# Output projection and first inner block of a two-layer diffusion step: other norm order, ScalarE copies, a third view, mask and sink

## The chip, the cores and the metric

The kernel runs on one core of one Trainium2 chip. TensorE (PE) multiplies, VectorE (DVE), ScalarE (ACT) and GpSimd (POOL) work elementwise, SyncE (SP) issues transfers. The metric is the device time of one execution in microseconds, median of several runs; the profile is of one execution more.

## The reference

One step of a two-layer backbone on 1024 latent tokens and 128 prompt tokens, width 1024, in float32. Layer 0 mixes tokens by differential attention (8 heads), layer 1 by sliding-window attention with a sink (16 heads in 4 groups); after each comes the output projection, a gated residual, and a SwiGLU feed-forward of 2816 inner columns. Cut to what the change touches:

```python
def post_norm_residual(x, y, g, gate):
    return x + gate * rmsnorm(y, g)

def pre_norm_modulate(x, g, shift, scale):
    return rmsnorm(x, g) * (1 + scale) + shift

def sink_softmax(s, sink):
    m = jnp.maximum(jnp.max(s, axis=-1, keepdims=True), sk)
    e = jnp.exp(s - m)
    return e / (jnp.sum(e, axis=-1, keepdims=True) + jnp.exp(sk - m))

ys = swa_latent_attention(...) @ w_o_swa[j]
xs = post_norm_residual(xs, ys, norm_g[i, 1], ms[2])
hs = pre_norm_modulate(xs, norm_g[i, 2], ms[3], ms[4])
y  = (jax.nn.silu(h @ w_gate) * (h @ w_up)) @ w_down
```

## The kernel before

Tokens stand in nine blocks of 128: eight latent ones and the prompt. Every float32 product is made of three matmuls on rounded parts: high x high, high x low, low x high. An operand is "split" by a cast (high) and a subtraction (low).

The order of instructions on each engine is the order of the code, which is written out by hand: a step function walks a tuple of actions, hooks put other work in between, and lists (`late`, `ahead`) say what follows which product. Each engine takes its own instructions in that order.

*Sliding-window attention* (`swa_attention`, from L981). At its start the mask is loaded (L986) and cast (L987), the identity cast (L989). A unit is one group of four heads and one token block. Per head: PE makes scores (L1014, L1017) and adds the mask by a matmul (L1020); VectorE takes the row maximum (L1025) and the minimum with the negated sink (L1026, 128x1); ScalarE takes the exponent (L1029); PE turns it (L1049); the turned tiles are split by ScalarE and VectorE, or, some of them, by POOL (rounding at L110, subtraction at L1072); PE multiplies by V (L1081, L1082).

*Output projection* (`OProj`, from L1237). `step(i)` handles five blocks at once at different ages: load x of block i, turn the heads of block i+1 (`turn`: PE transposes into PSUM, ScalarE copies them out, POOL rounds, VectorE subtracts, L1310 to L1316), statistics of the heads in layer 0 (L1263), the two halves of the projection of block i (`proj`, 24 matmuls each, L1324 to L1326, four PSUM tiles in turn), and for block i-1 the norms: `norms` 0 squares the projection, 1 makes the post-norm and the new x, stores x and squares it, 2 makes the pre-norm. The lines inside are those of helpers: L127 square with sum, L130 add, L135 root, L137 reciprocal, L153 and L154 post-norm, L145 and L146 pre-norm.

*Inner feed-forward blocks* (`Halves`, `Ffn`, `up`). The two halves of the input and the four of each weight are combined so that seven products per block of 128 inner columns do for gate and up: input combinations B11, B21, B22, T1 to T4 (`Halves`), weight combinations s0, s1 and so on (`prep`). The inputs of two token blocks form a pair: (0,4) and (1,5) make view 0 of 256 columns, (2,6), (3,7) and half of the prompt each side make view 1 of 320. `first` copies the turned first block out (ScalarE casts at L1393, VectorE copies at L1394), `second` makes the seven combinations of the second and splits them (L1404, L1407 are the helpers for high and low). `up` runs the inner blocks d = 0 to 21; d = 0 is written apart: seven products on view 0, with the pairs of view 1 prepared behind them, then seven on view 1. Each product is 12 matmuls (L1516 to L1518) into `guX`, `guY` or `guZ`, after which `sums` copies, adds and takes Silu (L1532 to L1553). `prep` for d = 0 is called by hooks at the last steps of the projection; there POOL makes s0 (L1468, L1469) and s1 (L1474, L1475) and the splits are at L1486 and L1488.

The lines that set the order in the projection and in the first block:

```python
for k, what, *arg in (
        (0, "load_x"), (1, "turn"), (3 - self.l, "load"), (-1, "norms", 0), (2, "stat", 0), (2, "stat", 1),
        (0, "proj", 0), *(((None, 0), (2, "scale")), ((None, 0), (2, "scale")))[self.l],
        (-1, "norms", 1), (-1, "norms", 2), (0, "proj", 1), (None, 1)):
...
late = [[], [lambda: step(pairs[0])], [lambda: step(pairs[0], 2), lambda: f.fetch(1)],
        [lambda: step(pairs[1])], [lambda: step(pairs[1], 2)], [], [lambda: step(pairs[2], 2)]]
```

Of the kernel before, what the change touches and what calls it, by code (L numbers as in the profile page):

```python
# [18 lines left out]
P = 128  # L19
# [25 lines left out]
def hybrid_step(ctx: ExitStack, tc: tile.TileContext, x_prompt, x_sample, cache_diff_k, cache_diff_v,  # L45
# [40 lines left out]
    negsink = const.tile([P, SH], F32, name="negsink")  # L86

# [354 lines left out]
    def small_params(sb):  # L442

        dma(out=subg, in_=diff_subln_g.rearrange("o p -> p o"))
# [536 lines left out]
    def swa_attention(op, wo_pool, pre, kv0, q0):  # L981
        with sbuf("sa") as sb, psum("sap") as ps:

            mask = sb.tile([P, 2, P], BF16, name="mask")
            mraw = sb.tile([P, 2, P], F32, name="mraw")
            dma(out=mraw, in_=swa_mask)  # L986
            act.copy(out=mask, in_=mraw)  # L987
            ident_b = sb.tile([P, P], BF16, name="ident_b")
            act.copy(out=ident_b, in_=ident)  # L989

            class Unit:
# [245 lines left out]
    class OProj:  # L1237
# [63 lines left out]
        def turn(self, tb):  # L1301
            i = OORDER.index(tb) % 2 * 2
            oh, ol = self.ohl[tb] = [self.room(f"w{i + f}", [P, KB, P], F32R, "oh") for f in range(2)]
            o32 = self.room("r1", [P, KB, P], F32, "o32")
# [23 lines left out]
        def norms(self, tb, part):  # L1328
# [4 lines left out]
            elif part == 1:  # L1333
# [3 lines left out]
                self.ss[tb] = sumsq([x], junk)  # L1337
# [24 lines left out]

    A_COLS = {(0, 0): ((0, 256, 0),), (0, 1): ((0, 256, 256),), (1, 0): ((0, 320, 512),),
              (1, 1): ((0, 256, 896), (256, 320, 832))}

    class Halves:
# [23 lines left out]
        def first(self, part, c, a, raw):  # L1390

            for i, name in enumerate(("B11", "B21")):
                act.copy(out=self.hi[name, part][:, :, c:c + a[i].shape[-1]], in_=a[i])  # L1393
                dve.tensor_copy(out=raw[:, i], in_=a[i])  # L1394

        def second(self, part, c, b, raws):
# [19 lines left out]
            high("B22", B22)  # L1416
            high("T2", T2)
            low("T3", T)
            dve.tensor_tensor(out=T, in0=B21, in1=T2, op=ALU.subtract)
            high("T4", T)  # L1420
            for name, x in (("B11", B11), ("B21", B21), ("T1", T1), ("T2", T2), ("B22", B22), ("T4", T)):
                low(name, x)
# [18 lines left out]
    class Ffn:  # L1441
# [18 lines left out]
        def prep(self, d, what):  # L1460
# [9 lines left out]
            elif what == "s1":  # L1470
# [3 lines left out]
                pool.tensor_tensor(out=s[:, 0:512], in0=A11, in1=A21, op=ALU.subtract)  # L1474
                pool.tensor_tensor(out=s[:, 512:D], in0=A12, in1=w[d, "r", "s0"][:, 512:D], op=ALU.subtract)  # L1475
            elif what == "u":
                u = w[d, "u"] = rooms.take((P, D), F32R, "fhl")
                act.copy(out=u[:, 0:512], in_=A22)
# [520 lines left out]
```

## Time and profile before

| | |
|---|---|
| median of 3 runs | 3180.54 us (3177.97 to 3180.6) |
| the profiled execution | 3179.54 us |
| its span | 3177.7 us |
| mean granted clock of PE | 0.982 |
| PE, DVE, ACT, POOL busy | 94%, 65%, 45%, 38% |

The profiled execution is 1.8 us longer than its span (start and end), and 1.0 us under the median. Stages follow each other: QKV product of layer 0 to 385 us, differential attention to 822, output projection to 968, up projection to 1500, down to 1795, then layer 1: QKV to 1960, sliding-window attention to 2234, output projection to 2366, up to 2891, down to the end. In a timeline row the columns are start, duration, engine, line, operation, output and inputs, shapes, and in brackets the idle time ahead of it with what ended it. The granted clock is a share of full speed: 1.00 is 2.4 GHz, the lower level 1.2 GHz.

### The profile page before, as it was taken

The page shows a single profiled execution, that of the slowest core. Times are in us where ns is not written, and L with a number is a line of the kernel's source. Part 1 is how long each engine was busy: PE and PEld are TensorE (multiplying, and loading weights), DVE is VectorE, ACT ScalarE, POOL GpSimd, SP SyncE. Part 2 cuts the span into 40 slices and gives each one's busy share as a digit, 9 for nine tenths or more (in the row PEclk, how much of TensorE's full clock was granted, in tenths as well). Part 3 has the DMA queues.
Part 4 walks back from the last instruction along what each step waited for, and adds up shares of the span by engine and source line. Part 5 has one row for each costly group of instructions (what it writes and reads, how often), then busy time and mean ns, then how long its engine had stood idle before and what let it go on. Part 6 is the DMA issues. An engine that isn't in the chain of part 4 may idle for free.

```text
span 3177.7 us, 47863 instructions
## 1 busy us (share of the span) xinstructions
PE 3000.0 (94%) x17998; PEld 2637.4 (83%) x17998; DVE 2070.7 (65%) x2849; ACT 1423.8 (45%) x2764; POOL 1215.6 (38%) x1120
## 2 busy tenths in 40 slices
PE   8999989988887999999999998999988999999999
PEld 5888777777776999999888787777768999998887
DVE  6786388888587777753786643999586633334544
ACT  6332267777554333333344323777443333333442
POOL 0453389999312444433000143666213434330000
PEclk9999999999898999999999999999999999999999
DMA  6675543332423343424865454433432322226664
GB/s 214 190 222 190 182 135 115 121 115 85 126 100 98 112 125 110 129 83 150 290 215 193 149 174 126 117 114 102 143 116 75 109 67 79 77 70 214 196 197 142
DMA packets 373807, 442.22 MB, mean 139 GB/s; under 512 B 26804, under 2 KB 295644, under 8 KB 373576
## 3 DMA queue, kind: packets, MB, share of 16 engines
q1 hardware_dynamic: 373576, 439.16, 43.9%
q8 instruction: 142, 2.33, 0.3%
q14 instruction: 89, 0.73, 0.1%
HBM read 335.71 MB, written 103.37 MB: 138 GB/s over the span
## 4 chain that ended last, share of the span: by engine, by line
PE 68%; POOL 13%; DVE 9%; ACT 4%; issue 3%; DMA 1%; SPq 1%; ACTq 0%; DVEq 0%; POOLq 0%
POOL aT L784 7%; PE guX L1516 6%; PE guX L1517 6%; PE guX L1518 6%; PE dacc L1633 6%; PE dacc L1635 6%; PE dacc L1634 6%; POOL aT L110 5%; PE qacc L556 4%; PE qacc L558 4%; PE qacc L557 4%; PE guY L1518 3%; PE guY L1516 3%; PE guY L1517 3%; PE guZ L1516 1%
## 5 line engine op out<-in xcount | busy, mean ns | idle before, releaser
L1633 PE MATMUL dacc<-fh,ahl 128*128 128x512 f32 x792 | 311.4, 393 | 2.4 <-DVE U L1552 2.4
L1635 PE MATMUL dacc<-fh,ahl 128*128 128x512 f32 x792 | 310.3, 392 | 0.0
L1634 PE MATMUL dacc<-fl,ahl 128*128 128x512 f32 x792 | 310.3, 392 | 0.0
L1549 POOL TENSOR_TENSOR sg<-sg,U 128x256 f32<-128x256 f32 x88 | 74.9, 851 | 576.2 <-ACT sg L1548 565.0
L556 PE MATMUL qacc<-whi,hh 128*128 128x512 f32 x648 | 259.3, 400 | 0.0
L558 PE MATMUL qacc<-whi,hl 128*128 128x512 f32 x648 | 254.3, 392 | 0.0
L557 PE MATMUL qacc<-wlo,hh 128*128 128x512 f32 x648 | 253.7, 391 | 0.6 <-DVE wlo L106 0.6
L617 POOL TENSOR_TENSOR qout<-t,t 128x512 f32<-128x512 f32 (+1 forms) x56 | 67.8, 1212 | 485.7 <-DVE vst L587 283.5
L784 POOL TENSOR_TENSOR aT<-a,aT 128x512 fp32r<-128x512 f32 x186 | 237.5, 1277 | 15.5
L1618 DVE TENSOR_TENSOR fl<-fraw,fh 128x1024 fp32r<-128x1024 f32 x132 | 161.7, 1225 | 118.6 <-ACT fh L1617 115.0
L744 DVE TENSOR_REDUCE nm<-S 128x1 f32<-128x1280 f32 x128 | 190.2, 1486 | 50.9 <-PE S L737 50.9
L1617 ACT CAST fh<-fraw 128x1024 fp32r<-128x1024 f32 x132 | 138.4, 1049 | 164.0 <-DMA fraw<-in_w_down_dram 157.4
L737 PE MATMUL S<-K,q 128*128 128x512 f32 (+1 forms) x768 | 184.5, 377 | 13.3 <-ACT e L749 9.2
L266 DVE SCALAR_TENSOR_TENSOR macc<-wmod,sc,macc 128x512 f32<-128x512 f32 x196 | 186.3, 994 | 0.0
L1633 PEld LDWEIGHTS dacc<-fh,ahl 128*128 128x128 f32 x792 | 148.7, 188 | 36.4 <-DVE U L1552 3.3
L1635 PEld LDWEIGHTS dacc<-fh,ahl 128*128 128x128 f32 x792 | 148.7, 188 | 33.5
L578 ACT CAST xT<-tpx 128x512 fp32r<-128x512 f32 x127 | 68.8, 591 | 240.2 <-issue 125.4
L1634 PEld LDWEIGHTS dacc<-fl,ahl 128*128 128x128 f32 x792 | 148.7, 188 | 32.8
L749 ACT ACTIVATE e<-S,nm 128x1280 f32<-128x1280 f32 x128 | 171.6, 1340 | 7.2 <-DVE nm L744 7.1
L737 PEld LDWEIGHTS S<-K,q 128*128 128x128 f32 x768 | 137.5, 193 | 44.3 <-ACT e L749 19.5
L110 POOL TENSOR_SCALAR aT<-a 128x512 fp32r<-128x512 f32 x192 | 154.2, 803 | 24.0 <-ACT a L773 24.0
L1488 DVE TENSOR_TENSOR fl<-fsum,fh 128x1024 fp32r<-128x1024 f32 x84 | 102.4, 1219 | 81.0 <-ACT fh L1486 81.0
(363 smaller groups left out, 9592.2 us busy)
## 6 DMA issues: line engine op xcount, KB each, us to landing
fraw<-in_w_down_dram SPq DMA_DIRECT2D x132, 512.0 KB
wmod<-in_w_mod_dram SPq DMA_DIRECT2D x112, 256.0 KB
araw<-a_d SPq DMA_DIRECT2D x132, 192.0 KB
fraw<-in_w_gate_dram SPq DMA_DIRECT2D x44, 512.0 KB
fraw<-in_w_up_dram SPq DMA_DIRECT2D x42, 512.0 KB
qT_d<-xT SPq DMA_DIRECT2D x36, 512.0 KB
q<-qT_d SPq DMA_DIRECT2D x64, 256.0 KB
wraw<-in_w_qkv_diff_dram SPq DMA_DIRECT2D x24, 512.0 KB
```

The costliest lines, as they stand in the source:

```text
L110: pool.tensor_scalar(out=out, in0=in_, scalar1=1.0, scalar2=0.0, op0=ALU.mult, op1=ALU.add)
L556: pe.matmul(acc, lhsT=xh, rhs=hi[:, a, :], start=(kb == 0), stop=False)
L557: pe.matmul(acc, lhsT=xh, rhs=lo[:, a, :], start=False, stop=False)
L558: pe.matmul(acc, lhsT=xl, rhs=hi[:, a, :], start=False, stop=(kb == KB - 1))
L737: pe.matmul(S[:, j:j + n], lhsT=self.q[:, f, m, i * P:(i + 1) * P], rhs=kv[self.h][0][:, m, j:j + n], start=(f == 0), stop=(f == 1))
L784: (dve if self.last else pool).tensor_tensor(out=lo, in0=x, in1=hi.bitcast(F32), op=ALU.subtract)
L1516: pe.matmul(o, lhsT=hi[:, kb, :], rhs=xh[:, kb, :], start=(first and kb == 0), stop=False, **more)
L1517: pe.matmul(o, lhsT=hi[:, kb, :], rhs=xl[:, kb, :], start=False, stop=False, **more)
L1518: pe.matmul(o, lhsT=lo[:, kb, :], rhs=xh[:, kb, :], start=False, stop=(kb == 3), **more)
L1633: pe.matmul(acc, lhsT=ah, rhs=hi[:, cs], start=(d == 0), stop=False)
L1634: pe.matmul(acc, lhsT=ah, rhs=lo[:, cs], start=False, stop=False)
L1635: pe.matmul(acc, lhsT=al, rhs=hi[:, cs], start=False, stop=(d == NDF - 1))
```

## The change

- *Norms.* `norms` has four parts. 0 and 1 stay one step behind the projection; the square of x (2) and the pre-norm (3) come at the start of the step after, two behind. Two more steps run at the end instead of code written out for the prompt.
- *Turn.* ScalarE writes the rounded high part straight from PSUM, VectorE subtracts it from PSUM; the copy o32 and POOL's rounding are gone.
- *Halves.* `first` only copies out, both copies on ScalarE; the casts of B11 and B21 stand in `second`, whose order changes.
- *Views.* In d = 0, view 1 of 320 columns is done as views of 256 and 64 columns; from d = 1 on nothing changes.
- *Prep.* For d = 0 VectorE makes s1 instead of POOL; hooks move; the fetch of d = 1 follows view 0.
- *Mask and sink.* Mask and bfloat16 identity are made with the small parameters in the QKV stage. The minimum with the sink takes the sink as a scalar operand.

```diff
     def small_params(sb):
+        mraw = junk[:, 0:2 * P].rearrange("p (a k) -> p a k", k=P)
+        dma(out=mraw, in_=swa_mask)
+        act.copy(out=mask, in_=mraw)
+        act.copy(out=ident_b, in_=ident)
...
-                    dve.tensor_tensor(out=nm, in0=nm, in1=negsink[:, hs:hs + 1], op=ALU.min)
+                    dve.tensor_scalar(out=nm, in0=nm, scalar1=negsink[:, hs:hs + 1], scalar2=None, op0=ALU.min)
...
         def turn(self, tb):
+                hi, lo = oh[:, ks, :], ol[:, ks, :]
                 if self.l == 0:
-                    act.activation(out=o32[:, ks, :], in_=tp, func=AF.Copy, scale=subg)
+                    act.activation(out=hi, in_=tp, func=AF.Copy, scale=subg)
+                    dve.scalar_tensor_tensor(out=lo, in0=tp, scalar=subg, in1=hi.bitcast(F32), op0=ALU.mult,
+                                             op1=ALU.subtract)
                 else:
-                    act.copy(out=o32[:, ks, :], in_=tp)
-                pool_round(oh[:, ks, :], o32[:, ks, :])
-                dve.tensor_tensor(out=ol[:, ks, :], in0=o32[:, ks, :], in1=oh[:, ks, :].bitcast(F32), op=ALU.subtract)
+                    act.copy(out=hi, in_=tp)
+                    dve.tensor_tensor(out=lo, in0=tp, in1=hi.bitcast(F32), op=ALU.subtract)
...
                 dma(out=x_d[tb * P:(tb + 1) * P, :], in_=x)
-                self.ss[tb] = sumsq([x], junk)
+            elif part == 2:
+                self.ss[tb] = sumsq([self.xt[tb]], junk)
...
-                    (0, "load_x"), (1, "turn"), (3 - self.l, "load"), (-1, "norms", 0), (2, "stat", 0), (2, "stat", 1),
-                    (0, "proj", 0), *(((None, 0), (2, "scale")), ((None, 0), (2, "scale")))[self.l],
-                    (-1, "norms", 1), (-1, "norms", 2), (0, "proj", 1), (None, 1)):
+                    (-2, "norms", 2), (-2, "norms", 3), (0, "load_x"), (1, "turn"), (3 - self.l, "load"),
+                    (-1, "norms", 0), (2, "stat", 0), (2, "stat", 1), (0, "proj", 0), (None, 0), (2, "scale"),
+                    (-1, "norms", 1), (0, "proj", 1), (None, 1)):
...
+    VIEWS = ((0, 0, 256), (1, 0, 320), (1, 0, 256), (1, 256, 320))
...
-            for i, name in enumerate(("B11", "B21")):
-                act.copy(out=self.hi[name, part][:, :, c:c + a[i].shape[-1]], in_=a[i])
-                dve.tensor_copy(out=raw[:, i], in_=a[i])
+            for i in range(2):
+                act.copy(out=raw[:, i], in_=a[i])
...
+            act.copy(out=B22, in_=b[1])
             dve.tensor_tensor(out=T1, in0=b[0], in1=B11, op=ALU.subtract)
-            act.copy(out=B22, in_=b[1])
             dve.tensor_tensor(out=T, in0=B22, in1=b[0], op=ALU.subtract)
+            high("B11", B11)
+            high("B21", B21)
             high("T1", T1)
...
-                pool.tensor_tensor(out=s[:, 0:512], in0=A11, in1=A21, op=ALU.subtract)
-                pool.tensor_tensor(out=s[:, 512:D], in0=A12, in1=w[d, "r", "s0"][:, 512:D], op=ALU.subtract)
+                eng = pool if d else dve
+                eng.tensor_tensor(out=s[:, 0:512], in0=A11, in1=A21, op=ALU.subtract)
+                eng.tensor_tensor(out=s[:, 512:D], in0=A12, in1=w[d, "r", "s0"][:, 512:D], op=ALU.subtract)
...
-                    for i, k in enumerate((0, 1, 2, 4, 3, 5, 6)):
-                        self.product(0, k, 0)
-                        for f in late[i] if i < len(late) else ():
-                            f()
-                    for k in range(7):
-                        self.product(0, k, 1)
-                        self.free(0, k)
-                        self.ahead(1, k)
+                    for view in (0, 2, 3):
+                        for i, k in enumerate((0, 1, 2, 4, 3, 5, 6)):
+                            self.product(0, k, view)
+                            if view == 3:
+                                self.free(0, k)
+                            for f in late.get((view, i), ()):
+                                f()
...
-                hooks[8, 0] = [lambda: prep("s0", "hg")]
-                hooks[8, 1] = [lambda: prep("s1", "lg")]
-                for i in range(-2, NTB):
+                hooks[8, 0] = [lambda: prep("s0", "hg", "lg")]
+                hooks[9, 0] = [lambda: prep("ha", "s1", "la")]
+                hooks[9, 1] = [lambda: prep("hb", "lb")]
+                for i in range(-2, NTB + 2):
...
+                late = {(0, 1): [pair(0)], (0, 4): [pair(0, 2)], (0, 5): [pair(1)],
+                        (0, 6): [pair(1, 2), lambda: f.fetch(1)], (2, 1): [pair(2, 2)],
+                        (2, 3): prep("s0"), (2, 4): prep("s1"), (2, 6): prep("hg"),
+                        (3, 1): prep("lg", "ha"), (3, 3): prep("la", "hb"), (3, 5): prep("lb"),
+                        (3, 6): prep("u") + [lambda: f.fetch(2)]}
```

The order on VectorE at the end of the projection of layer 0, where the last pair of view 0 ends and the post-norm of the block before the last follows. Before (K is the room of x, `oh` the low part of the turned heads, `xn` the normed block):

```order
L1407 TENSOR_TENSOR T2l<-raw,T2h 128x4x128
L1407 TENSOR_TENSOR B22l<-raw,B22h 128x4x128
L1407 TENSOR_TENSOR T4l<-raw,T4h 128x4x128
L1316 TENSOR_TENSOR oh<-o_9452,oh 128x512 x2
L130 TENSOR_TENSOR ss<-ss 128x1
L137 RECIPROCAL rs<-ss 128x1
L153 SCALAR_TENSOR_TENSOR xn<-oacc,rs,q 128x512 x2
L154 TENSOR_TENSOR K<-xn,K 128x1024
L137 RECIPROCAL rs<-ss 128x1
L145 SCALAR_TENSOR_TENSOR xn<-K,rs,bc 128x1024
L146 TENSOR_TENSOR xn<-xn,bc 128x1024
```

And now (the lines are shifted: L148 and L149 are the pre-norm, L156 and L157 the post-norm, L1312 the subtraction in `turn`):

```order
L1410 TENSOR_TENSOR T1l<-raw,T1h 128x4x128
L1410 TENSOR_TENSOR B22l<-raw,B22h 128x4x128
L1410 TENSOR_TENSOR T4l<-raw,T4h 128x4x128
L140 RECIPROCAL rs<-ss 128x1
L148 SCALAR_TENSOR_TENSOR xn<-K,rs,bc 128x1024
L149 TENSOR_TENSOR xn<-xn,bc 128x1024
L1312 SCALAR_TENSOR_TENSOR oh<-tp_o,subg,oh 128x512 x2
L133 TENSOR_TENSOR ss<-ss 128x1
L140 RECIPROCAL rs<-ss 128x1
L156 SCALAR_TENSOR_TENSOR xn<-oacc,rs,q 128x512 x2
L157 TENSOR_TENSOR K<-xn,K 128x1024
```

The pre-norm that followed a block's own post-norm now stands ahead of the next block's post-norm, and the subtraction of the heads reads PSUM.

The order on ScalarE in view 0 of layer 0, before (`s` and `U` are copies of sums out of PSUM, `fh` and `fhl` weight casts):

```order
L1486 CAST fh<-V 128x1024
L135 ACTIVATE ss<-ss,eps_t 128x1
L1532 COPY s_9709<-guX 128x256
L127 ACTIVATE junk,ss<-K 128x1024
L135 ACTIVATE ss<-ss,eps_t 128x1
L1478 CAST fhl<-V 128x512
L1393 CAST B11h<-tp_n 128x4x128
L1393 CAST B21h<-tp_n 128x4x128
L1537 COPY U_9752<-guX 128x256
L1538 ACT_TABLE_LOAD
L1538 ACTIVATE s_9709<-s_9709 128x256
```

And now:

```order
L1543 COPY s_9687<-guX 128x256
L138 ACTIVATE ss<-ss,eps_t 128x1
L1496 CAST fh<-K 128x1024
L1397 COPY raw<-tp_n 128x512 x2
L1548 COPY U_9728<-guX 128x256
L1549 ACT_TABLE_LOAD
L1549 ACTIVATE s_9687<-s_9687 128x256
L130 ACTIVATE junk,ss<-K 128x1024
L138 ACT_TABLE_LOAD
L138 ACTIVATE ss<-ss,eps_t 128x1
L1552 COPY U_9743<-guX 128x256
L1488 CAST fhl<-V 128x512
```

The casts straight from the turned tile became raw copies, and between Silu and the U copy stands a square and a root with a table load each way.

## Rows read from the trace of the kernel before

**Rows 1.** The page, part 1: busy time, share and instructions of each engine.

```profile
PE 3000.0 (94%) x17998; PEld 2637.4 (83%) x17998; DVE 2070.7 (65%) x2849; ACT 1423.8 (45%) x2764; POOL 1215.6 (38%) x1120
```

**Rows 2.** Table by stage: stretch, length, PE PEld DVE ACT POOL busy, clock, DMA, GB/s.

```profile
840.00:970.00 130.00, 115.92 (x546) 94.82 (x546) 99.59 (x164) 72.09 (x213) 19.45 (x17) 0.93 0.35 115
...
970.00:1030.00 60.00, 40.09 (x245) 38.19 (x245) 42.25 (x63) 26.12 (x49) 12.56 (x12) 0.83 0.25 77
...
1030.00:1500.00 470.00, 469.54 (x3503) 464.64 (x3503) 310.19 (x355) 157.53 (x297) 199.52 (x161) 1.00 0.38 115
...
1970.00:2234.00 264.00, 245.28 (x1663) 203.16 (x1664) 236.09 (x465) 198.16 (x468) 169.74 (x191) 0.99 0.37 109
...
2368.00:2430.00 62.00, 40.67 (x264) 39.09 (x265) 43.88 (x66) 25.81 (x49) 16.60 (x14) 0.83 0.25 76
```

**Rows 3.** Timeline of PE, output projection, both layers (idle before, releaser).

```profile
934.12 1.97 PE L1386 MATMUL tp_n<-ident,xn 128*128 128x128 f32 x8 [3.11 <-DVE raw L1394]
...
954.84 0.77 PE L1324 MATMUL oacc<-woh,oh 128*128 128x512 f32 x1 [4.49 <-DVE xn L153]
...
2353.26 0.76 PE L1324 MATMUL oacc<-woh,oh 128*128 128x512 f32 x1 [5.16 <-DVE xn L153]
```

**Rows 4.** Timeline of PE, first inner block of both layers.

```profile
977.37 0.89 PE L1386 MATMUL tp_n<-ident,xn 128*128 128x128 f32 x4 [4.24 <-DVE s L1534]
...
1009.37 0.63 PE L1517 MATMUL guX<-B11l,fh 128*128 128x320 f32 x1 [8.84 <-DVE B11l L1407]
...
2407.98 0.64 PE L1517 MATMUL guX<-B11l,fh 128*128 128x320 f32 x1 [9.39 <-DVE B11l L1407]
```

**Rows 5.** Timeline of VectorE and POOL, end of projection and first block, layer 0.

```profile
940.55 0.16 DVE L137 RECIPROCAL rs<-ss 128x1 f32<-128x1 f32 x1 [1.54 <-ACT ss L135]
...
948.32 1.10 DVE L1407 TENSOR_TENSOR T2l<-raw,T2h 128x512 fp32r<-128x512 f32 x1
...
950.36 1.75 DVE L1407 TENSOR_TENSOR T4l<-raw,T4h 128x512 fp32r<-128x512 f32 x1
...
992.20 0.68 DVE L1407 TENSOR_TENSOR T4l<-raw,T4h 128x512 fp32r<-128x512 f32 x1
...
947.92 1.98 POOL L110 TENSOR_SCALAR oh<-o 128x512 fp32r<-128x512 f32 x2 [18.05 <-ACT o L1312]
...
968.57 2.31 POOL L1474 TENSOR_TENSOR K<-fraw,V 128x512 f32<-128x512 f32 x1 [10.06 <-DMA x_d<-K]
```

**Rows 6.** Chain of waits at 256 and 320 columns; timeline of eight 128-column transposes.

```profile
2423.02 0.12 PE guX L1516
...
2424.24 0.15 PE guX L1517
...
1959.10 0.85 PE L577 MATMUL tpx<-ident_r,st 128*128 128x128 f32 x8 [1.37 <-DVE st L565]
```

**Rows 7.** Timeline of ScalarE, first block of layer 0.

```profile
983.46 1.28 ACT L1538 ACT_TABLE_LOAD   x1
```

**Rows 8.** Timeline: first masked score; ScalarE at the small parameters.

```profile
1965.15 0.26 PE L1020 MATMUL S<-mask,ident_b 128*128 128x128 bf16 x1 [4.67 <-ACT mask L987]
...
191.10 0.20 ACT L453 ACTIVATE le<-le 128x2 f32<-128x2 f32 x1 [4.91 <-DVE le L452]
```

**Rows 9.** Groups by form, attention 1972 to 2230; then timeline of one wait.

```profile
L1014 PE MATMUL S<-K,q 128*128 128x256 f32 x246 | 56.7, 312 | 16.9 <-ACT e L1029 16.8
...
2024.57 1.27 POOL L1072 TENSOR_TENSOR pT<-a,pT 128x512 fp32r<-128x512 f32 x1
...
2024.73 1.12 DVE L1026 TENSOR_TENSOR nm<-nm,negsink 128x1 f32<-128x1 f32 x1
...
2026.78 0.38 PE L1014 MATMUL S<-K,q 128*128 128x256 f32 x1 [1.43 <-ACT e L1029]
```

**Rows 10.** Two source lines on VectorE: shortest, median and longest ns, starts, form.

```profile
L264 DVE TENSOR_SCALAR macc<-wmod,sc x28: 469/1402/1520, 1025.8 to 2472.0; 128x512 f32<-128x512 f32 x28
...
L755 DVE RECIPROCAL s<-s x64: 145/152/156, 402.1 to 801.6; 128x1 f32<-128x1 f32 x64
```

More of the change, by code (lines that the diff above doesn't have):

```diff
@@ L86, in hybrid_step @@
     negsink = const.tile([P, SH], F32, name="negsink")
+    mask = const.tile([P, 2, P], BF16, name="mask")
+    ident_b = const.tile([P, P], BF16, name="ident_b")
     def sbuf(name, side=None):
@@ L982, in swa_attention @@
         with sbuf("sa") as sb, psum("sap") as ps:
[L984 to L989, printed above, removed]
             class Unit:
@@ L1415, in second @@
             high("T3", T)
-            high("B22", B22)
             high("T2", T2)
+            low("B11", B11)
             low("T3", T)
             dve.tensor_tensor(out=T, in0=B21, in1=T2, op=ALU.subtract)
+            high("B22", B22)
             high("T4", T)
-            for name, x in (("B11", B11), ("B21", B21), ("T1", T1), ("T2", T2), ("B22", B22), ("T4", T)):
+            for name, x in (("B21", B21), ("T2", T2), ("T1", T1), ("B22", B22), ("T4", T)):
                 low(name, x)
@@ L1473, in prep @@
                 s = w[d, "r", "s1"]
-                pool.tensor_tensor(out=s[:, 0:512], in0=A11, in1=A21, op=ALU.subtract)
-                pool.tensor_tensor(out=s[:, 512:D], in0=A12, in1=w[d, "r", "s0"][:, 512:D], op=ALU.subtract)
+                eng = pool if d else dve
+                eng.tensor_tensor(out=s[:, 0:512], in0=A11, in1=A21, op=ALU.subtract)
+                eng.tensor_tensor(out=s[:, 512:D], in0=A12, in1=w[d, "r", "s0"][:, 512:D], op=ALU.subtract)
             elif what == "u":
-                u = w[d, "u"] = rooms.take((P, D), F32R, "fhl")
-                act.copy(out=u[:, 0:512], in_=A22)
-                dve.tensor_tensor(out=u[:, 512:D], in0=A22, in1=u[:, 0:512].bitcast(F32), op=ALU.subtract)
+                if (d, "u") not in w:
+                    u = w[d, "ur"] = rooms.take((P, D), F32R, "fhl")
+                    w[d, "u"] = u[:, 0:512], u[:, 512:D]
+                hi, lo = w[d, "u"]
+                act.copy(out=hi, in_=A22)
+                dve.tensor_tensor(out=lo, in0=A22, in1=hi.bitcast(F32), op=ALU.subtract)
                 rooms.give(w[d, "r", 1])
@@ L1498, in product @@
             to, i, half, name = self.PRODUCTS[k]
-            n = PARTS[part]
-            acc = self.acc
+            src, c0, c1 = VIEWS[part]
+            n, acc = c1 - c0, self.acc
             first = k in (0, 1, 3)
@@ L1509, in product @@
             if i == 1:
-                hi, lo = [self.w[d, "u"][:, f * 512:(f + 1) * 512] for f in range(2)]
+                hi, lo = self.w[d, "u"]
             else:
@@ L1513, in product @@
             hi, lo = [x.rearrange("p (a n) -> p a n", n=P) for x in (hi, lo)]
-            xh, xl = self.hv.hi[name, part], self.hv.lo[name, part]
+            xh, xl = [x[name, src][:, :, c0:c1] for x in (self.hv.hi, self.hv.lo)]
             for kb in range(4):
@@ L1523, in post @@
             t = self.pt.tile([P, 320], F32, name=name, tag=name, bufs={"s1": 3, "sg": 3 - self.l}.get(name, 2))
-            return t[:, 0:PARTS[part]]
+            return t[:, 0:VIEWS[part][2] - VIEWS[part][1]]
         def sums(self, d, k, part):
-            acc, t, n = self.acc, self.sums_of.setdefault(part, {}), PARTS[part]
+            acc, t = self.acc, self.sums_of.setdefault(part, {})
+            n = VIEWS[part][2] - VIEWS[part][1]
             X, Y, Z = [acc[to, part][:, 0:n] if (to, part) in acc else None for to in "XYZ"]
@@ L1563, in free @@
             elif k == 6:
-                self.rooms.give(self.w[d, "u"])
+                if (d, "ur") in self.w:
+                    self.rooms.give(self.w[d, "ur"])
         def begin(self, rooms):
@@ L1757, in pair @@
                 rooms = [where[f"x{OORDER.index(tb) % 5}"] for tb in tbs]
-                yield from f.hv.pair(part, c, [op.xn[tb] for tb in tbs], [*rooms, *self.temps][:3])
+                temps = self.temps + [where["x4"]]
+                yield from f.hv.pair(part, c, [op.xn[tb] for tb in tbs], [*rooms, *temps][:3])
                 if part:
-                    f.rooms.free += rooms
+                    f.rooms.free += [r for r in rooms if r != where["x4"] or len(tbs) == 1]
+                    if len(tbs) == 1:
+                        f.rooms.free.append(where["x4"])
                 yield
@@ L1787, in begin @@
                 hooks[7, 0] = [first]
[L1788 to L1797 removed]
+                hooks[8, 0] = [lambda: prep("s0", "hg", "lg")]
+                hooks[9, 0] = [lambda: prep("ha", "s1", "la")]
+                hooks[9, 1] = [lambda: prep("hb", "lb")]
+                for i in range(-2, NTB + 2):
+                    if i == NTB:
+                        f.rooms.free = [where["w0"], where["w1"], where["r1"], self.temps[0]]
+                    op.step(i, hooks)
                 f.rooms.free += [where["b0"], where["b1"]] + [where["b2"]] * l
@@ L1814, in ffn, with pair, prep @@
                 R.tile([P, 512], F32, name="room", tag="mw", bufs=2)
-                self.temps = [macc, (R, "mw", 2)]
+                self.temps = [macc]
                 pt = high.enter_context(sbuf(f"pt{l}", "right"))
                 pairs = [self.pair(1, c, *tbs) for c, tbs in ((0, (2, 6)), (P, (3, 7)), (2 * P, (TB_PROMPT,)))]
-                late = [[], [lambda: step(pairs[0])], [lambda: step(pairs[0], 2), lambda: f.fetch(1)],
-                        [lambda: step(pairs[1])], [lambda: step(pairs[1], 2)], [], [lambda: step(pairs[2], 2)]]
+                def pair(i, n=1):
+                    return lambda: step(pairs[i], n)
+                def prep(*whats):
+                    return [lambda what=what: f.prep(1, what) for what in whats]
+                late = {(0, 1): [pair(0)], (0, 4): [pair(0, 2)], (0, 5): [pair(1)],
[3 more added lines that the diff above has]
+                        (3, 6): prep("u") + [lambda: f.fetch(2)]}
                 def switch():
```

10 lines of the change are left out of this document (2 added, 8 removed).

## Prediction

> **What bounds the kernel now.** I read the page first: TensorE (PE) is busy 94% of the span [rows 1]. A change can therefore gain in two ways only: by removing places where PE stands idle, or by removing places where it runs at its lower clock. The table by stage shows where these are [rows 2]. From the second inner block on, the up projection has 469.54 us of PE work in 470.00, so nothing is to be had there. The first inner block of layer 0 with the end of the output projection ahead of it (970 to 1030) has 40.09 of 60.00 at a mean granted clock of 0.83; that of layer 1 (2368 to 2430) has 40.67 of 62.00, also at 0.83. The sliding-window attention (1970 to 2234) has 245.28 of 264.00 at 0.99. The projection of layer 0 (840 to 970) runs at 0.93. These are the stages that the diff touches.
>
> Next, the timeline of PE in the projections: before the last token block it waits 4.49 us in layer 0 and 5.16 us in layer 1 for VectorE's `xn`, and in layer 0 once more 3.11 us for the raw copies [rows 3]. In the first block the large waits are for `s` of VectorE (4.24 in layer 0), for raw copies, and, largest, 8.84 and 9.39 in the two layers for the prompt's B11 remainder, since view 1 of 320 columns cannot begin without the prompt's 64 [rows 4].
>
> **The projection: norms in four links, the turned heads straight from PSUM.** The pre-norm moves behind the next block's work, so VectorE no longer stands between the two norms until ScalarE has squared and rooted x: 1.54 us per step [rows 5]. POOL's rounding of the heads goes (two in 1.98), and with it the stretch of VectorE operations beside it: T4l took 1.75 beside POOL and 0.68 alone, T2l 1.10, and B22l behind it as much [rows 5], together 1.1 + 0.4 + 0.4 = 1.9. That is 3.4 us ahead of a wait of 4.49 or 5.16. The raw copies leave VectorE as well, so in layer 1 I take 4.3 of 5.16; in layer 0 ScalarE has eight statistics per block besides, and now the raw copies and the split casts in the same queue, so I take 1.5 of 4.49, and 2 of the 3.11. Sum 7.8, with ends 0 (the wait passes to ScalarE's `oh`) and 12.8 (all three). With shorter waits the lower clock shrinks: 130 us at 0.93 lack 9 us of full speed in layer 0 [rows 2], layer 1 is nearly at full speed there; I take 6, ends 0 and 9. **Together 14.**
>
> **The first block in three views.** *More matmuls.* The 320 columns of view 1 become 256 and 64: 84 matmuls per layer of 320 columns go, 84 of 256 and 84 of 64 come. Start to start the trace has 0.12 us for 256 columns and 0.145 for 320 at full clock [rows 6]. It has no 64-column matmul on this path; the nearest are the 128-column transposes, eight in 0.85 us, which is 0.106 [rows 6]. Bounds are 0.06 (in proportion to the columns, from 128) and 0.12 (no dearer than 256). I take 0.106, as the weights are as many. Cost 84 x (0.12 + 0.106 - 0.145) = 6.8 us per layer, **-14** for both (ends 6 and 16). *Waits.* View 2 needs pairs (2,6) and (3,7) and not the prompt, so the 8.84 and 9.39 should shrink; but pair (3,7)'s chain still has to end and PE has only view 0 to do meanwhile, so I leave 2.5 in each: +13. The four sums `s1` move from POOL to VectorE. On POOL the first waited for the store of x and took 2.31 [rows 5]; on VectorE they stand ahead of `s`, on which PE's transposes wait. A 128x512 VectorE operation is 0.68 there. I take +1.5 for both layers. *Tables.* ScalarE now goes back to the root's table and again to Silu's inside view 0: two loads more per layer at 1.28 [rows 7]. One of the two stands in PE's way, I judge: -2.5. *Clock.* PE is busy 40.1 us in a window whose work is worth some 31 at full speed (84 x 0.12 + 84 x 0.145 and five turned blocks at 0.85 make 26.5 for the block, the rest is the second block's): some 9 us per layer go to the 1.2 GHz level. With shorter gaps I take back 5 of these 18. Sum 13 + 1.5 + 5 - 14 - 2.5 = **+3**; ends -14 (no wait goes) and +25 (all of 41 idle less the new matmuls).
>
> **The mask.** Before, the first score waits 4.67 us for ScalarE's cast of the mask, which itself waits for the load [rows 8]. Some 0.5 of it is left to the identity's cast and its weight load, so 4.1 us go; what is late next is the first exponent, which was late anyway. **+4**, ends 0 and 5. Load and casts move to the first QKV product. There ScalarE now waits for the mask's load ahead of the other small parameters; it already stood 4.91 us in that place for them [rows 8], and I cost it at nothing (4 if that cover is gone). The fetch of the first gate weights passes two loads of o on SP's queue, the next up weights come earlier, the down stage's loads change places; those stages have PE full, so nothing, with 2 us as the other end.
>
> **The sink.** In the sliding-window stage PE waits 16.9 us before L1014 for ScalarE's exponent [rows 9]. The timeline shows one of some twelve such waits: POOL starts a 1.27 us operation at 2024.57, VectorE's 128x1 minimum with the sink starts at 2024.73 and lasts until POOL has ended, 1.12, where a 128x1 reciprocal needs 0.15 [rows 9, 10]; the exponent and then the score follow, and PE stands 1.43. As `tensor_scalar` the operation has one tensor in SBUF and a scalar. Is it also held? Nearest by kind is L264, a tensor_scalar of 512 columns: 0.47 at the least, 1.40 at the median, so that one is held. Nearest by size is the 128x1 reciprocal, also one tensor: 0.156 at the most in 64 [rows 10]. I take the row nearest in size. Gain 12 x (1.12 - 0.15) = 11.6, less what stays where such a wait was shorter or the exponent is late by itself: **+9**, ends 0 and 14.
>
> The Trainium skill speaks against this. Its page "VectorE: DVE Perf Modes", section "What auto-detection actually checks", lets a one-source operation between SBUF tensors use both ports when the outermost dimension is even or equal on both sides, and "SBUF — State Buffer" makes such an operation wait for the port pair it shares with GpSimd. A 128x1 operation would fit that rule and gain nothing; L264's row agrees with it, no row shows the 128x1 form.
>
> **Sum.** 14 + 3 + 4 + 9 = 30 from the profiled execution's 3179.5 us (span 3177.7 and 1.8 around it): 3149.5, and since the median of the runs lies 1.0 above, **3150.5**. A difference under 0.2%, or 6.4 us, can't be told from none.
>
> **Rivals.** *(a) The sink's operation is still held by POOL.* For it: L264. Against it: the reciprocals. All else as above: 3150.5 + 9 = 3159.5. *(b) ScalarE becomes the bound of the first block.* Raw copies, all seven casts of a pair, the U copies of three views and four table loads stand in one queue; the waits for VectorE become waits for ScalarE. For it: an even alternation of casts and subtractions was there before, with ScalarE waiting for VectorE; against it: ScalarE is busy under half of this window. The +3 becomes about -9, and the sink works half the time: 3150.5 + 12 + 4 = 3166. *(c) Slower: the clock stays at 1.2 GHz through all three views.* The block's matmuls are some 34 us at full speed, so 68 at half, against 56 now from first product to the second block: 12 more per layer, 24 in all, while the projection's gain loses its 6 of clock and is 8, the mask 4, and the sink nothing: 3180.5 + 24 - 12 = 3192. It decides when the block grows by more than 6 us per layer. For it: each wait in this block was followed by a stretch at the low level; against it: the largest wait shortens. *(d) Everything clears:* projection 20, block 8, mask 4, sink 12: 3136.
>
> **How the numbers follow.** Forecast 0.43, (a) 0.28, (b) 0.13, (c) 0.08, (d) 0.08. The range goes from (d) to somewhat past (b): 3136 to 3171. Faster takes the forecast, (a), (d) and nearly all of the nearer part of (b), less a little for mishaps in the costs: 0.84; the rest of (b) and near cases of (c) give 0.08 the same; 0.08 slower.
>
> **What would show it.** Sink: VectorE's minimum beside POOL's L1072 near 0.15 and the idle before L1014 near 6 us; else it stands near 1.0 as before. Mask: no wait of 4 us near 1961 and the scores right behind the ident_b cast. Projection: waits before the last `oacc` under 3 us in layer 0 and 1 us in layer 1. Block: from its first product to the second block's some 55 us in each layer, with 64-column matmuls 0.10 to 0.11 apart, and the wait before view 2 under 3 us. I am wrong if the block takes over 60 us, or if PE waits for ScalarE's casts where it waited for VectorE's.

## The result and the profile after

The changed kernel takes 3159.3 us (median of 4 runs, 3157.87 to 3162.34) against 3179.6 for the kernel before; the ratio is 0.9938 with a 95% interval of 0.9921 to 0.9955, some 20 us less. 3150.5 was forecast, within 3136 to 3171: the time lies in the range, 8.8 us above the forecast. The profiled execution took 3157.87 us, its span is 3156.1, so 21.6 less than the span before.

The table by stage, first of the changed kernel, then of the kernel before with the stages cut at the same places (the first matmul of each: output projection, first inner block, second inner block; in the middle the sliding-window attention). Columns as in [rows 2].

```profile
819.20:955.20 136.00, 126.06 (x610) 103.48 (x609) 97.47 (x172) 80.14 (x238) 3.46 (x2) 0.96 0.46 140
955.20:1016.60 61.40, 46.55 (x293) 43.86 (x292) 38.02 (x59) 30.42 (x61) 10.12 (x9) 0.79 0.24 77
1016.60:1498.70 482.10, 481.64 (x3572) 476.51 (x3572) 314.75 (x362) 162.08 (x304) 201.77 (x164) 1.00 0.38 115
1955.40:2212.20 256.80, 246.31 (x1683) 206.21 (x1682) 219.83 (x471) 202.06 (x474) 168.78 (x191) 0.99 0.42 123
2212.20:2339.90 127.70, 122.87 (x610) 99.96 (x609) 85.51 (x143) 58.99 (x125) 3.81 (x4) 1.00 0.43 138
2339.90:2400.50 60.60, 45.79 (x294) 43.31 (x292) 38.51 (x60) 31.40 (x66) 9.40 (x9) 0.77 0.28 89
```

```profile
822.40:968.70 146.30, 131.36 (x609) 107.58 (x608) 105.34 (x177) 77.81 (x234) 21.45 (x21) 0.92 0.42 131
968.70:1025.10 56.40, 35.82 (x210) 33.69 (x209) 41.33 (x60) 25.06 (x48) 11.17 (x9) 0.82 0.23 73
1025.10:1504.90 479.80, 479.34 (x3571) 474.21 (x3570) 314.72 (x362) 162.15 (x304) 203.09 (x164) 1.00 0.39 117
1959.80:2233.80 274.00, 249.58 (x1683) 206.70 (x1683) 238.89 (x471) 201.64 (x476) 169.54 (x191) 0.98 0.40 116
2233.80:2366.10 132.30, 124.40 (x611) 102.70 (x609) 93.61 (x149) 58.62 (x124) 17.71 (x22) 0.97 0.44 137
2366.10:2422.50 56.40, 33.53 (x209) 31.75 (x208) 42.29 (x61) 24.75 (x48) 11.07 (x9) 0.82 0.25 78
```

Read the length of each stage and PE's busy time behind it. The projections lost 10.3 and 4.6 us, the attention 17.2. **The first inner blocks grew** by 5.0 and 4.2: their idle time fell (56.40 - 35.82 = 20.6 to 61.40 - 46.55 = 14.8 us in layer 0, 22.9 to 14.8 in layer 1), but PE's busy time rose by 10.7 and 12.3. The second inner block and what follows grew by some 2 us more in layer 0, though their matmuls were not changed. Stages with no change in them differ by up to 3 us between executions in both directions, with stretches at the low clock in other places: the differential attention ended 3 us earlier here, the QKV product of layer 1 took 1.8 longer. So single executions are compared below by the stage that an edit touches. How far one stage differs by itself is seen where its code is the same: the change, and the runs below with small matmuls, with the sink as a tensor and with the mask late, took 135.2 to 136.3 and 126.3 to 127.7 us in the projections of the two layers, 61.4 to 63.0 and 59.8 to 62.5 in the first blocks.

The waits that answer to [rows 3, 4], in the changed kernel's PE timeline:

```profile
942.40 0.47 PE L1324 MATMUL oacc<-woh,oh 128*128 128x512 f32 x1 [3.09 <-DVE xn L156]
...
971.48 1.38 PE L1390 MATMUL tp_n<-ident,xn 128*128 128x128 f32 x8 [2.90 <-ACT raw L1413]
...
977.84 1.97 PE L1390 MATMUL tp_n<-ident,xn 128*128 128x128 f32 x8 [3.55 <-ACT raw L1397]
...
982.46 0.58 PE L1527 MATMUL guX<-B11l,fh 128*128 128x256 f32 x1 [0.88 <-DVE B11l L1410]
...
2328.66 0.47 PE L1324 MATMUL oacc<-woh,oh 128*128 128x512 f32 x1 [1.73 <-DVE xn L156]
```

The last projection waits 3.09 and 1.73 instead of 4.49 and 5.16; the 8.84 before the second view's second matmul has become 0.88. Most of the waiting in the block of layer 0 is now put down to ScalarE (ACT). What costs is behind them, in view 3. Its stretch by stretch, layer 0 (view 3 begins at 1001.2, the second inner block at 1016.6):

```profile
1001.20:1004.40 3.20, 3.20 (x32) 3.20 (x30) 0.75 (x3) 0.79 (x3) 0.74 (x2) 0.99 0.25 82
1004.40:1016.60 12.20, 11.90 (x57) 11.76 (x57) 3.52 (x4) 2.88 (x7) 0.32 (x1) 0.50 0.25 71
1016.60:1021.60 5.00, 5.00 (x23) 5.00 (x23) 2.72 (x4) 0.37 (x1) 4.21 (x4) 0.52 0.35 98
1021.60:1030.00 8.40, 8.40 (x66) 8.40 (x65) 3.37 (x5) 3.39 (x7) 1.62 (x2) 1.00 0.07 17
```

PE is busy in nearly all of it, and yet the granted clock falls from 2.4 to 1.2 GHz after 3.2 us of 64-column matmuls and stays there until 5 us into the next block. View 3 takes 15.4 us where 84 x 0.106 = 8.9 was counted on (13.1 in layer 1).

In the attention, the first masked score stands without a wait ahead, where it had 4.67 before [rows 8]:

```profile
1955.96 0.23 PE L1019 MATMUL S<-mask,ident_b 128*128 128x128 bf16 x1
```

The load and the casts cost nothing where they are now: the QKV stage ends at 390.1 us, before at 390.4. The sink's line and one of its uses beside POOL (the group by source line: shortest, median, longest ns; then the timeline):

```profile
L1025 DVE TENSOR_SCALAR nm<-nm,negsink x128: 212/214/217, 1957.0 to 2202.1; 128x1 f32<-128x1 f32 x128
```

```profile
2024.16 1.29 POOL L1071 TENSOR_TENSOR pT<-a,pT 128x512 fp32r<-128x512 f32 x1
...
2025.19 0.21 DVE L1025 TENSOR_SCALAR nm<-nm,negsink 128x1 f32<-128x1 f32 x1
```

It takes 0.21 us in all 128 cases, also where POOL is at work until 2025.45. Of the 128, 47 start inside a POOL operation that has at least 0.25 us to go; they take 212 to 216 ns. Before, 57 started so and took 0.27 to 1.12.

### The profile page after: what moved, and what is told of

It is laid out like the page before. It is cut to its first block, busy times and chain, and to the rows that moved or that the text cites. A ratio compares the mean times of both kernels' runs of the same rounds, so it can differ in the third digit from the quotient of the medians.

```text
span 3156.1 us, 48188 instructions
## 1 busy us (share of the span) xinstructions
PE 3012.5 (95%) x18166; PEld 2652.0 (84%) x18166; DVE 2027.9 (64%) x2839; ACT 1440.0 (46%) x2798; POOL 1176.1 (37%) x1084
## 5 line engine op out<-in xcount | busy, mean ns | idle before, releaser
L1560 POOL TENSOR_TENSOR sg<-sg,U 128x256 f32<-128x256 f32 (+2 forms) x90 | 76.0, 845 | 633.8 <-ACT sg L1559 527.4
```

## The experiments

Lengths of a stage run from its first matmul to that of the next one; "block" is the first inner block up to the second. All are edits of the changed kernel unless said otherwise.

**Two views again**

```diff
-                    for view in (0, 2, 3):
+                    for view in (0, 1):
...
-                        (0, 6): [pair(1, 2), lambda: f.fetch(1)], (2, 1): [pair(2, 2)],
+                        (0, 6): [pair(1, 2), lambda: f.fetch(1), pair(2, 2)] + prep("s0"),
...
```

> The change with its first block back in two views of 256 and 320 columns (the prompt is prepared at the end of view 0, the weights of the next block behind view 1's products); everything else of the change stays. In the changed kernel the first block takes 61.4 and 60.5 us, and its 64-column matmuls run at the 1.2 GHz level for 12 of 15.4 us in layer 0 and 6 of 13 us in layer 1. Theory (the third view itself is the loss: more matmuls, and small ones that PE runs at the low level): the block falls to 50 to 55 us in each layer though a wait of some 8 to 10 us for the prompt's B11 remainder returns, the start of the up projection loses its 2 us at the low level, and the time is 3138 to 3150. Rival (the new waits for ScalarE's copies are the loss and the third view pays by hiding the prompt): the block stays at 60 us or grows, 3157 to 3168.

Measured: 3138.06 us, ratio to before 0.9868 (0.9851 to 0.9884). Blocks 54.6 and 53.3 us, and the up projection behind them at 479.9 and 474.3 as before the change. The theory holds: the third view is the loss, about 9 us in each layer. The wait for the prompt returned, in two parts:

```profile
989.27 0.63 PE L1526 MATMUL guX<-B11h,fh 128*128 128x320 f32 x1 [3.34 <-ACT B11h L1407]
...
995.47 0.64 PE L1527 MATMUL guX<-B11l,fh 128*128 128x320 f32 x1 [5.56 <-DVE B11l L1410]
```

The blocks of both layers as a whole:

```profile
956.60:1011.30 54.70, 36.82 (x210) 34.19 (x209) 38.58 (x57) 30.71 (x61) 9.20 (x7) 0.72 0.27 86
...
2330.20:2383.50 53.30, 35.55 (x210) 32.88 (x209) 38.22 (x57) 30.76 (x60) 8.81 (x7) 0.78 0.30 95
```

PE stands idle for 17.9 and 17.8 us here, for 14.8 in both layers of the change. So the third view saved only 3 us of waiting per layer: it takes away the prompt's 8.9 and brings other waits in view 2, in layer 0 before the prompt's transposes (2.56) and before the next product (1.30). It cost 9.7 and 10.2 us of PE's busy time, and some 2 us more in the second block.

**Small matmuls where nothing waits**

```diff
+    FILL = {(5, 0): (64, 84), (10, 0): (128, 84), (15, 0): (192, 84)}
...
+            o = self.acc["X", 1][:, 320:320 + cols]
+            for i in range(n):
+                pe.matmul(o, lhsT=hi[:, i % 4, :], rhs=xh[:, i % 4, 0:cols], start=(i == 0), stop=(i == n - 1),
+                          skip_group_check=True)
...
```

> The change, with matmuls put in for measuring in the up projection of layer 0, where PE has had no wait for a long time: 84 of 64 columns inside inner block 5, 84 of 128 columns in block 10, 84 of 192 columns in block 15, into columns of the X accumulators that nothing reads. Theory A (small matmuls draw the clock down by themselves): the granted clock falls to 0.5 within the 84 of 64 columns, which then take well over 9.2 us, and comes back behind them; less so or not at all at 128 and 192. Rival B (the clock in the third view is an after-effect of the waits ahead of it): all 84 of 64 columns are 0.11 us apart, 9.2 us, clock 1.00 throughout. Either way the time rises by 26 to 36 us in all.

The added matmuls begin a new sum in a bank where X is still being summed, so X is not the reference's in these three blocks. Measured: 3199.21 us in one run, 39.9 more than the change and so more than the 26 to 36 expected. By stretch (64 columns from 1122.0 to 1137.0, 128 in the row of 1254.65, 192 in the last):

```profile
1115.00:1122.00 7.00, 6.43 (x50) 6.17 (x48) 6.54 (x7) 2.66 (x6) 5.28 (x4) 1.00 0.18 57
1122.00:1126.00 4.00, 4.00 (x34) 4.00 (x34) 0.77 (x2) 1.24 (x2) 0.00 (x0) 0.93 0.22 66
1126.00:1130.00 4.00, 4.00 (x21) 4.00 (x20) 0.00 (x0) 0.00 (x0) 0.00 (x0) 0.50 0.00 0
1130.00:1134.00 4.00, 4.00 (x20) 4.00 (x21) 0.00 (x0) 0.00 (x0) 0.00 (x0) 0.50 0.01 4
1134.00:1137.00 3.00, 3.00 (x16) 2.92 (x16) 0.00 (x0) 0.00 (x0) 0.00 (x0) 0.50 0.00 0
1254.65:1264.25 9.60, 9.60 (x85) 9.60 (x86) 1.57 (x2) 2.20 (x3) 0.00 (x0) 1.00 0.10 29
1378.50:1388.10 9.60, 9.59 (x85) 9.54 (x86) 0.79 (x2) 1.26 (x2) 0.00 (x0) 1.00 0.09 27
```

Theory A holds for the clock: among 64-column matmuls it falls to 1.2 GHz, and 84 of them take 14.8 us. At 128 and at 192 columns it stays at 1.00 (9.4 and 9.5 us for 84). The same single wait of 0.57 us stands ahead of all three sets, so the wait is not what tells them apart. And from start to start, 64, 128 and 192 columns cost the same at full clock, 0.11 us each: of these widths the narrower ones save nothing.

**The third view wider**

```diff
-    VIEWS = ((0, 0, 256), (1, 0, 320), (1, 0, 256), (1, 256, 320))
+    VIEWS = ((0, 0, 256), (1, 0, 320), (1, 0, 192), (1, 192, 320))
...
```

> The change with its second and third view cut otherwise: 192 and 128 columns instead of 256 and 64, so the third view holds half of pair (3,7) beside the prompt; as many matmuls as in the change, and 128 columns took 0.114 us each at full clock inside an inner block where 64 columns took 0.179. Theory (not the number of matmuls but the low clock that the 64 columns draw is the larger loss): from the third view on PE stays at full clock, the first block takes 53 to 57 us in both layers, the up projection behind it loses its 2 us, the time is 3142 to 3152. Rival (the number of matmuls or the order of the waits is the loss): the block stays at 60 us or more, 3156 or more.

Measured: 3145.61 us in one run. From 1005.6 on, where the third view begins, the clock is 1.00, and the next block starts at full speed (the first and the last row are the blocks of both layers as a whole):

```profile
957.00:1015.50 58.50, 43.95 (x294) 41.37 (x292) 39.00 (x60) 31.28 (x65) 9.96 (x9) 0.80 0.25 82
...
1005.00:1010.00 5.00, 4.72 (x43) 4.58 (x41) 1.87 (x4) 2.25 (x5) 1.02 (x2) 1.00 0.15 43
1010.00:1015.50 5.50, 5.43 (x49) 5.43 (x49) 2.47 (x3) 2.23 (x6) 0.46 (x1) 1.00 0.34 100
1015.50:1495.40 479.90, 479.44 (x3572) 474.31 (x3572) 314.63 (x362) 161.93 (x304) 201.85 (x164) 1.00 0.39 116
2332.00:2389.80 57.80, 43.54 (x293) 41.07 (x292) 38.32 (x60) 31.35 (x65) 9.26 (x9) 0.79 0.27 89
```

The blocks take 58.5 and 57.8, a little over the 53 to 57 expected, and the 2 us behind them are gone: 5.1 and 4.3 us against the change, with the waits nearly as long (14.6 and 14.3 us of idle time). With two views it was 9. So about half of the third view's 9 us is the low clock that came with the 64 columns. The other half, 3.9 and 4.5 us, is what as many more matmuls cost (7.1 and 8.0 us of busy time against two views) beyond the waiting that the third view saves (3.3 and 3.5).

**The sink as a tensor operation**

```diff
-                    dve.tensor_scalar(out=nm, in0=nm, scalar1=negsink[:, hs:hs + 1], scalar2=None, op0=ALU.min)
+                    dve.tensor_tensor(out=nm, in0=nm, in1=negsink[:, hs:hs + 1], op=ALU.min)
```

> The change with the sink's minimum as an operation on two tensors again. Theory (the scalar form does not wait for POOL, and that is where most of the attention's 17 us come from): 128x1 minima up to 1.1 us return beside POOL, PE's waits before the scores return at 1.0 to 1.5, twelve of them, the sliding-window stage grows by 9 to 12 us. Rival (the stage gained by the mask and the clock): under 4 us.

Measured: the attention takes 267.8 us, 11.0 more than in the change. The source line and PE's group before the scores (busy and mean, then idle before):

```profile
L1025 DVE TENSOR_TENSOR nm<-nm,negsink x128: 159/237/1121, 1958.9 to 2215.1; 128x1 f32<-128x1 f32 x128
...
L1013 PE MATMUL S<-K,q 128*128 128x256 f32 x256 | 58.9, 311 | 19.9 <-ACT e L1028 19.8
```

In the change that group reads:

```profile
L1013 PE MATMUL S<-K,q 128*128 128x256 f32 x254 | 58.6, 312 | 8.9 <-ACT e L1028 8.8
```

The theory holds, and the 11.0 us are just these waits: 14 of them last 0.95 us or more, 2 in the change.

**The mask late**

```diff
...
         with sbuf("sa") as sb, psum("sap") as ps:
+            mraw = sb.tile([P, 2, P], F32, name="mraw")
+            dma(out=mraw, in_=swa_mask)
+            act.copy(out=mask, in_=mraw)
+            act.copy(out=ident_b, in_=ident)
```

> The change with the mask loaded and cast, and the identity cast, at the start of the sliding-window attention again. Theory: a wait of 4 to 5 us for the mask returns before the first masked score, and the sliding-window stage grows by 4 to 7 us, the rest beyond 4 from the clock after the wait. Rival (something else is late there by now, such as the exponent): under 2 us.

Measured: the attention takes 262.4 us, 5.6 more, as the theory has it, and the wait is back, a little longer than expected:

```profile
1965.50 0.26 PE L1019 MATMUL S<-mask,ident_b 128*128 128x128 bf16 x1 [5.35 <-ACT mask L988]
```

**Sink and mask alone, on the kernel before** (the same two edits, nothing else):

> The kernel before with two parts of the change only: the sink's minimum in scalar form, mask and identity made with the small parameters. Theory (these two make 11.0 and 5.6 us and depend on nothing else in the change): the sliding-window stage falls from 274 to 256 to 259 us, all else as before, 3161 to 3166; so the rest of the change, projection and first block together, is worth only 2 to 6 us. Rival (part of the gain comes through the rest): 3168 or more.

Measured: 3163.36 us, ratio 0.9948 (0.9931 to 0.9965); the attention takes 256.3. The theory holds: these two parts make nearly the whole result. Projection and first block together bring 4.1 us (3163.4 to 3159.3); the intervals of the two ratios overlap, so it isn't shown that this differs from nothing.

**Norms in the step of the post-norm**

```diff
-                    (-2, "norms", 2), (-2, "norms", 3), (0, "load_x"), (1, "turn"), (3 - self.l, "load"),
+                    (0, "load_x"), (1, "turn"), (3 - self.l, "load"),
...
-                    (-1, "norms", 1), (0, "proj", 1), (None, 1)):
+                    (-1, "norms", 1), (-1, "norms", 2), (-1, "norms", 3), (0, "proj", 1), (None, 1)):
```

> The change with the square of x and the pre-norm back in the step of the post-norm, directly behind it. Theory (the links carry the projections' gain: VectorE no longer stands until ScalarE has squared and rooted x): PE's waits in the output projection grow by 3 to 5 us in each layer, the time by 5 to 12 with the clock, the first block unchanged within 3. Rival (the heads' split out of PSUM carries it): under 2 us in each layer.

Measured: 3176.1 us in one run, 16.8 more than the change where 5 to 12 were expected. The projection of layer 0 grows by 4.9 us, 3.7 of it idle time, as the theory has it; that of layer 1 not at all (-0.7), as the rival has it. The blocks, which were to stay as they are, grow by 5.1 and 3.8. So the links are worth as much in the first block, where without them new waits stand behind ScalarE's weight cast, among others:

```profile
978.82 0.58 PE L1526 MATMUL guY<-T3h,fh 128*128 128x256 f32 x1 [1.95 <-ACT fh L1496]
...
2366.29 0.39 PE L1526 MATMUL guY<-T3h,fh 128*128 128x256 f32 x1 [3.61 <-ACT fh L1496]
```

**Heads rounded on POOL**

```diff
...
-                    act.copy(out=hi, in_=tp)
-                    dve.tensor_tensor(out=lo, in0=tp, in1=hi.bitcast(F32), op=ALU.subtract)
+                    act.copy(out=o32[:, ks, :], in_=tp)
+                pool_round(oh[:, ks, :], o32[:, ks, :])
+                dve.tensor_tensor(out=ol[:, ks, :], in0=o32[:, ks, :], in1=oh[:, ks, :].bitcast(F32), op=ALU.subtract)
```

> The change with the turned heads copied out, rounded on POOL and subtracted from the copy again, as before. Theory (this half of the projections' gain is POOL's hold on VectorE, 1.9 us a step, and a longer way from the transposes to the split heads): waits of 1 to 4 us in each layer's projection return. Rival (the norms alone carry it): under 1 us.

Measured: 3160.9 us in one run. The projections grow by 1.7 and 2.4 us, the blocks fall by 0.8 and 0.9. Both projections lie 1.4 us or more above all four runs of the change's own code (137.7 and 130.1), so something came back; but only 0.9 and 0.8 of it is waiting, which is the rival's size, and the rest is longer busy time. Over the whole kernel it can't be told from nothing.

**Raw copies on VectorE**

```diff
-            for i in range(2):
-                act.copy(out=raw[:, i], in_=a[i])
+            for i, name in enumerate(("B11", "B21")):
+                act.copy(out=self.hi[name, part][:, :, c:c + a[i].shape[-1]], in_=a[i])
+                dve.tensor_copy(out=raw[:, i], in_=a[i])
```

> The change with the first block of each pair copied out as before: B11 and B21 cast by ScalarE straight from PSUM, the raw copies by VectorE. Theory (in the changed first block ScalarE's queue is what the pairs wait for, 2.9 + 3.5 + 1.2 us in layer 0 on its copies and casts): the block falls by 2 to 5 us in each layer. Rival (VectorE would be later still, with the s1 sums in its queue): the block grows by 1 to 4 us, and the projection of layer 0 gets its 3 us wait for the raw copies back.

Measured: 3173.1 us in one run; the blocks grow by 4.1 and 2.6 us. My theory fell. ScalarE is named in front of PE's waits in the change, but with the copies on VectorE PE's idle time is longer, 17.5 and 16.7 us against 14.8 in both layers. The longest waits of layer 0:

```profile
971.73 0.58 PE L1525 MATMUL guX<-T1h,fh 128*128 128x256 f32 x1 [5.67 <-ACT U L1547]
985.14 1.11 PE L1390 MATMUL tp_n<-ident,xn 128*128 128x128 f32 x4 [4.33 <-DVE raw L1398]
```

The rival's 3 us in the projection of layer 0 did not come back, though (0.85 before that block's heads, 0.91 in the change).

**A version that beats both.** In the kernel with two views the longer part of the prompt's wait, 5.56, stands behind three subtractions of VectorE at 1.75 to 1.76 each, beside four sums of POOL for inner block 1.

```diff
-                eng = pool if d else dve
+                eng = pool if d > 1 else dve
...
+                eng = dve if d == 1 else pool
```

> The kernel of e1_two_views with the four weight sums of inner block 1 on VectorE, behind the prompt's pair, instead of POOL, where three subtractions of VectorE ahead of the prompt's B11 remainder took 1.76 instead of 0.69 beside them. Theory (PE's wait of 5.56 and 4.27 us before view 1's second matmul is that hold): these waits fall by 2.5 to 3.5 us, the block to 50 to 52 us in both layers, the time to 3129 to 3136. Rival (the chain of the prompt's casts on ScalarE ends no earlier, or VectorE's four sums delay the next subtraction that PE needs): the block stays at 53 us or more, 3136 to 3142.

Measured: 3133.02 us, ratio to before 0.9849 (0.9834 to 0.9864), in the middle of what was expected. The wait is 2.12 in both layers, down by 3.4 and 2.2, and the blocks take 47.7 and 50.5 (layer 0 shorter than the 50 to 52 expected):

```profile
990.17 0.64 PE L1527 MATMUL guX<-B11h,fh 128*128 128x320 f32 x1 [3.33 <-ACT B11h L1407]
...
992.93 0.63 PE L1528 MATMUL guX<-B11l,fh 128*128 128x320 f32 x1 [2.12 <-DVE B11l L1410]
```

It is 26 us better than the change, with all of the change but the third view and the place of the four sums. Against two views alone it is 5.0 us, with intervals that overlap.

## Why the time lay in the range, and which step failed

| part | forecast | measured | by |
|---|---|---|---|
| projection, waits and clock | -14 | -14.9 | stages (10.3 + 4.6) |
| first block, and what it does behind | -3 | +12.9 | stages (5.0 + 4.2, then 2.2 + 1.5) |
| mask | -4 | -5.6 | mask late |
| sink | -9 | -11.0 | sink as tensor |
| sum | -30 | -18.6 | span -21.6, the rest in stages not touched and 0.6 in the attention |

The time lies in the range, but not because every part came as forecast. The first block missed by 15.9 us; the other three parts gained 4.5 more than forecast, and 3.0 came from stages not touched and from the attention. That these made up for half of the miss is luck. Two of the prediction's own signs of being wrong came up: the block takes over 60 us in both layers, and PE waits for ScalarE where it waited for VectorE (10.3 of 14.8 us in layer 0, 0.5 of 20.5 before).

*Projection.* Waits were to fall by 7.8; idle time fell by 5.0 (146.3 - 131.4 to 136.0 - 126.1) and 3.1 us, 8.1. The rest came from the clock, 0.92 to 0.96 and 0.97 to 1.00, as thought. The waits before the last `oacc` came out just longer than the signs named, 3.09 and 1.73 for 3 and 1. The split was less right: the links alone are worth 4.9 us in layer 0 and nothing in layer 1, the turn 1.7 and 2.4. And of the 1.9 us that the prediction puts down to the stretch beside POOL's rounding, 1.07 stood beside another operation. T4l began at 950.36 [rows 5], the rounding had ended at 949.90, and POOL was at a weight sum:

```profile
949.87 1.69 POOL L1468 TENSOR_TENSOR V<-V 128x512 f32<-128x512 f32 x1
```

In the change this sum runs at 927.79, and T4l takes 0.69.

*Sink.* The 128x1 operation goes with the reciprocal of its size, not with the 512-column operation of its kind [rows 10]. Rival (a), which needed it held, did not happen, and the time came within 0.2 us of its 3159.5 for another reason. The Trainium skill's rule in "VectorE: DVE Perf Modes", section "What auto-detection actually checks", lets an operation with a single source take the mode on two ports when source and destination are in SBUF with outermost non-unit dimensions both even or equal. The prediction left out "non-unit"; one element per partition has no such dimension, so the rule doesn't say what holds for it. The measurement decides, 212 to 217 ns in all 128 cases: it isn't held. Unhindered it takes longer than before, 0.21 instead of 0.16.

*Mask.* The 4.67 went entirely. With the mask late the stage is 5.6 us longer, the wait in it 5.35; how the 5.6 come about beyond the 4.1 that the prediction priced was not taken apart.

*First block: the step that failed is the clock.* Term by term, for both layers:

- Waits: they were to fall by 13 + 1.5 - 2.5 = 12 and fell by 13.8 (5.7 + 8.1). But the third view, for which the 13 were counted, has only 5.9 of that (two views against the change); the rest of the change brought 7.8. The sum is right by another split.
- Matmuls: 14 were forecast. "I take 0.106, as the weights are as many": that is the price at full clock, and there it is right, 0.11. With 192 and 128 columns, as many more matmuls cost 15.1 against two views.
- Clock: it was to give back 5, so that busy time would rise by 9 net. It rose by 23.0 (10.7 + 12.3). Of this, 4.9 is what the 64 columns cost beyond the run with 192 and 128, where view 3 stays at 1.00, and 3.7 more were lost in the second block before the clock came back. The 5 given back weren't there either, with or without 64 columns: with two views, and so with as many matmuls as before, PE's busy time is 72.4 us in both blocks, 68.4 in the last version, and 69.4 before.

Rival (c) had named a low clock, but through all views, and argued it from the waits; the runs with added matmuls and with 128 columns show another cause, the 64-column matmuls themselves, with no more wait ahead than wider ones had that stayed at full clock.

*Rival (b)*, ScalarE as the bound of the block, has PE's waits named after ScalarE on its side (2.90 and 3.55), but these waits aren't where the block lost, since idle time fell, and giving the copies back to VectorE made the block longer. I take it that the pair's chain over both engines bounds those waits; no run isolates it.

## What to carry to other kernels

Before cutting matmuls to hide a wait, price the pieces: here pieces of 64, 128 and 192 columns cost 0.11 us alike, and among pieces of 64 PE's clock fell to half, for themselves and for what followed. And see what wait comes next: of the prompt's 8.9 us, 3 were saved. Compare idle and busy time of a stage separately before and after: the waits can fall as planned while the work gets dearer by more. And a step on VectorE with one element per partition, beside long POOL operations, is better written with its second operand as a scalar: here 0.21 us each time, instead of 0.16 to 1.12.

## What I had not expected of the hardware

PE's granted clock fell to 0.50 while PE was busy without a break, on 64-column matmuls (84 in 14.8 us), and not on the 128- and 192-column ones (84 in 9.4 and 9.5 us). A 128x1 `tensor_scalar` between SBUF tensors is not held by a POOL operation (0.21 us in all 128 cases), while the 128x512 one of the same kind is: the 18 of L264's 28 that start inside a POOL operation take 1.10 to 1.52 us, the other ten 0.47 to 0.49 [rows 10].
